# An empty step of a lane moved from behind a tile's second scores to ahead of its first, in a hybrid encoder layer on one Trainium2 core

## The chip, the cores and the metric

The kernel runs on one core of a Trainium2 chip. The core has a matrix engine (TensorE, PE in the profile; its weight loads are PEld), a vector engine (VectorE, DVE), a scalar engine (ScalarE, ACT), a general engine (GpSimd, POOL) and one that issues transfers (SyncE, SP). Each works through its own list of instructions in order and waits at semaphores for the others. The metric is the device time of one execution in microseconds, lower is better; the time before is the median of three runs.

## The reference

One layer of a bidirectional hybrid encoder, for two request groups (1024 and 256 rows, together ten tiles of 128 rows) with shared weights, in float32:

```
hn = rms_norm(x, norm_g);  proj = hn @ w_in
xbc, z_ssd, dt, q, k, v, z_att, mq, z_mem = split(proj)
# 1. state space group: convolution of width 5 over time, silu, two scans (forward and backward)
xbc   = silu(conv5(xbc));  y = scan(xbc, dt) + scan(reversed) + d_skip * xs
o_ssd = rms_norm(y * silu(z_ssd))
# 2. local attention: 8 heads in 2 key groups, |t - s| <= 128, linear distance penalty, a sink logit
s     = (rms_norm(q) . rms_norm(k)) * d**-0.5 - slope * |t - s|
o_att = softmax_with_sink(s) @ v * silu(z_att)
# 3. attention over a memory of 256 rows
o_mem = softmax(rms_norm(mq) . mk) @ mv * silu(z_mem)
out   = x + concat[o_ssd, o_att, o_mem] @ w_out
```

The changed code is part 2.

## The kernel before, in words

**Two kinds of work.** The large projections are split into two reduced-precision halves and run as three matmuls each. They run in blocks (`block_tok`, lines 258 to 260, one matmul 128 x 512; `block_feat`, lines 293 to 295, one matmul 128 x 320). Everything between the projections (local attention `attn`, memory attention, the scans `ssd_up` and `ssd_down`) is written as Python generators that stand in two queues, the lanes: `attn` in lane 0, the scans in lane 1.

**What sets the order.** After each unit of a projection block, `pump` adds the block's rates to what each lane is owed, and for every whole step owed it advances the generator at the lane's head to its next `yield`. A `yield` with nothing ahead of it is an empty step: it lets the projections and the other lane go on. A step's instructions are put into the program behind the last split of a weight tile (`marks`). The order on each engine follows from there by a list scheduler; at run time each engine keeps it. `some_left` puts in the taps of the convolution one at a time in the same way.

**Local attention, `attn(t)`, t = 0 to 9.** Tiles 0 to 3 run beside the `x` blocks (`block_feat`), which also produce the convolution's input; tile 4 beside the second `q` block, 5 to 7 beside further `block_tok` blocks, 8 and 9 later. One call norms its query tile `q`, splits it (`qh`), turns it by four matmuls per half into a PSUM tile `pq` (L671), and ACT copies that out as `qT` (L673); there are two, one for each half of the heads. Then a step issues the load of the gate `z`, and the four head pairs follow:

- `scores(rr)`: two score tiles `psc`, each of two matmuls (L689 and L690); DVE adds the distance penalty and takes the row minimum (L691, `lg` and `nm`); ACT takes the exponential (L695); DVE the reciprocal and the scaling (L697, L698).
- `turn_(rr)`: PE transposes the two scaled tiles into `ppt` (L628), after a small POOL memset that opens them as `lgw` (L635); ACT copies them out as `pT` (L713).
- `values()`: the product with the values.

**Buffers.** `pq`, `psc`, `ppt` and the small tiles of the scans share the PSUM pool `mix` with three buffers. The projections use the pool `acc` with five.

**The convolution's buffers.** For each pair of feature blocks, `ev_conv` opens a buffer `u`: DVE copies the carried columns in (L391) and clears the gaps (L392, L393). Taps run on ACT and DVE (L357, L362), then ACT's L365 and DVE's L368 finish `u`, and SyncE stores it (L372 and L373, to `xbc_d`). The tag of these buffers has two of them, so the next `u` opens over a stored one.

## Time and profile before

| what | value |
|---|---|
| median of 3 runs | 1779.43 us (1779.38 to 1779.74) |
| the profiled execution | 1784.13 us |
| its span | 1782.4 us, 31990 instructions, mean clock of PE 0.999 |
| PE busy | 1766.5 us (99%) |
| DVE busy | 1247.7 us (70%) |
| ACT busy | 919.5 us (52%) |
| POOL busy | 554.6 us (31%) |
| transferred | 301.16 MB, mean 169 GB/s |

The span is the time between the first and last instruction of the profiled execution; its own time includes what lies around the span. The busy time of PE is the sum over its matmuls, and what is missing to the span are its waits. In rows of the timeline the first number is the start in us from the span's start, the second the duration; in brackets stand the idle time of the engine ahead of it and what ended it. In rows of waits the numbers are the total, how often, and the longest, in us.

### The profile page before, as it was taken

How to read it: one execution, taken by the hardware profiler on the slowest of the kernel's cores; microseconds unless marked ns; L12 is line 12 of the kernel's file. 1: busy time of each engine (PE TensorE's matmuls, PEld its weight loads, DVE VectorE, ACT ScalarE, POOL GpSimd, SP SyncE). 2: the span in 40 equal slices, each digit the busy share in tenths (PEclk: the TensorE clock that was granted, in tenths of full speed). 3: DMA queues.
4: the chain of work that ended last, by engine and by line, in shares of the span. 5: the costliest groups of instructions: out<-in, count | busy, mean ns of one | idle time of the engine just before them, and what ended most of it. 6: DMA issues, size and time to landing. Idle time of an engine off the chain costs nothing. (4 is left out here: it accounts for less than half of the span.)

```text
span 1782.4 us, 31990 instructions
## 1 busy us (share of the span) xinstructions
PE 1766.5 (99%) x11046; PEld 1610.4 (90%) x11046; DVE 1247.7 (70%) x2348; ACT 919.5 (52%) x2049; POOL 554.6 (31%) x980
## 2 busy tenths in 40 slices
PE   9999999999999999999999999999999999999999
PEld 7888999999998999999889988887988888899999
DVE  5595788888868878777765675557777654766665
ACT  5554555554434766666455565645447533533333
POOL 0105798999810100001000100011110000058775
PEclk9999999999999999999999999999999999999999
DMA  9553444445446644553545655557777764644442
GB/s 303 189 183 114 146 149 145 144 141 169 123 145 202 191 136 131 150 168 98 182 121 187 181 160 160 165 170 246 220 244 236 247 191 145 220 142 148 148 142 78
DMA packets 208210, 301.16 MB, mean 169 GB/s; under 512 B 19568, under 2 KB 86192, under 8 KB 208048
## 3 DMA queue, kind: packets, MB, share of 16 engines
q1 hardware_dynamic: 207904, 299.06, 54.6%
q8 instruction: 87, 1.43, 0.3%
q14 instruction: 75, 0.61, 0.1%
q10 hardware_dynamic: 144, 0.06, 0.0%
HBM read 236.36 MB, written 62.69 MB: 168 GB/s over the span
## 5 line engine op out<-in xcount | busy, mean ns | idle before, releaser
L207 DVE TENSOR_TENSOR wl<-wraw,wh 128x512 fp32r<-128x512 f32 (+1 forms) x480 | 347.2, 725 | 229.4 <-ACT wh L206 212.5
L206 ACT ACTIVATE wh<-wraw 128x512 fp32r<-128x512 f32 (+1 forms) x480 | 292.1, 613 | 291.8 <-PE acc L260 156.1
L258 PE MATMUL acc<-wh,xH 128*128 128x512 f32 (+1 forms) x1088 | 418.9, 385 | 0.4 <-DVE v_all L337 0.4
L259 PE MATMUL acc<-wl,xH 128*128 128x512 f32 (+1 forms) x1088 | 410.4, 377 | 0.2
L260 PE MATMUL acc<-wh,xL 128*128 128x512 f32 (+1 forms) x1088 | 410.6, 378 | 0.0
L258 PEld LDWEIGHTS acc<-wh,xH 128*128 128x128 f32 x1088 | 204.6, 188 | 37.3 <-issue 2.7
L260 PEld LDWEIGHTS acc<-wh,xL 128*128 128x128 f32 x1088 | 204.8, 188 | 36.7 <-issue 0.2
L259 PEld LDWEIGHTS acc<-wl,xH 128*128 128x128 f32 x1088 | 204.9, 188 | 36.3 <-DVE wl L207 1.5
L293 PE MATMUL acc<-xH,wh 128*128 128x320 f32 x640 | 202.5, 316 | 0.6 <-DVE zs L309 0.6
L206 ACT ACTIVATE sh<-ws 128x384 fp32r<-128x384 f32 x176 | 91.5, 523 | 210.6 <-POOL ws L1256 111.1
L295 PE MATMUL acc<-xH,wl 128*128 128x320 f32 x640 | 199.1, 311 | 0.0
L294 PE MATMUL acc<-xL,wh 128*128 128x320 f32 x640 | 198.1, 310 | 0.0
L207 DVE TENSOR_TENSOR sl<-ws,sh 128x384 fp32r<-128x384 f32 x176 | 124.9, 713 | 97.0 <-ACT sh L206 94.7
L1256 POOL TENSOR_TENSOR ws<-wraw 128x128 f32<-128x128 f32 x176 | 112.8, 641 | 205.9 <-DMA wraw<-in_w_in_pairs_dram 93.7
L293 PEld LDWEIGHTS acc<-xH,wh 128*128 128x128 f32 x640 | 120.2, 188 | 3.6 <-issue 2.4
L1256 POOL TENSOR_TENSOR ws<-wraw,ws 128x128 f32<-128x128 f32 x176 | 117.9, 670 | 13.8
L294 PEld LDWEIGHTS acc<-xL,wh 128*128 128x128 f32 x640 | 120.2, 188 | 1.3 <-issue 1.0
L295 PEld LDWEIGHTS acc<-xH,wl 128*128 128x128 f32 x640 | 120.2, 188 | 0.7 <-issue 0.7
L1256 POOL TENSOR_TENSOR ws<-ws,wraw 128x128 f32<-128x128 f32 x176 | 117.1, 665 | 0.0
L1256 POOL TENSOR_TENSOR wraw<-wraw 128x128 f32<-128x128 f32 x176 | 111.4, 633 | 13.7
L635 POOL MEMSET lgw<- 128x1 f32 x40 | 3.9, 98 | 310.4 <-DVE lg L698 202.4
L362 DVE SCALAR_TENSOR_TENSOR c<-u,vec,c 128x638 f32<-128x638 f32 (+1 forms) x96 | 90.1, 940 | 9.0 <-ACT c L357 8.7
(440 smaller groups left out, 3957.5 us busy)
## 6 DMA issues: line engine op xcount, KB each, us to landing
wraw<-in_w_in_laid_dram SPq DMA_DIRECT2D x176, 256.0 KB, 2.9
wraw<-in_w_in_pairs_dram SPq DMA_DIRECT2D x112, 256.0 KB, 2.7
wraw<-in_w_out_laid_dram SPq DMA_DIRECT2D x64, 256.0 KB, 3.2
wraw<-in_w_out_pairs_dram SPq DMA_DIRECT2D x64, 256.0 KB, 2.7
rf<-ac SPq DMA_DIRECT2D x40, 256.0 KB, 3.9
rb<-ac SPq DMA_DIRECT2D x40, 256.0 KB, 4.9
wraw<-in_w_mem_laid_dram SPq DMA_DIRECT2D x32, 256.0 KB, 4.7
xst<-in_x_sample_dram SPq DMA_DIRECT2D x20, 256.0 KB, 5.0
```

Source lines behind the costliest of these rows:

```text
L206: a = A.activation(h, raw, AF.Copy)
L207: b = V.tensor_sub(l, raw, h.bitcast(F32))
L258: T.matmul(ps[t][:, :n], sh, h[:, :n], start=(k_ == 0), stop=False)
L259: T.matmul(ps[t][:, :n], sh, l[:, :n], start=False, stop=False)
L260: T.matmul(ps[t][:, :n], sl, h[:, :n], start=False, stop=(k_ == KT - 1))
L293: T.matmul(o, sh, cur["H", q][:, m, c], start=(k == 0), stop=False)
L294: T.matmul(o, sh, cur["L", q][:, m, c], start=False, stop=False)
L295: T.matmul(o, sl, cur["H", q][:, m, c], start=False, stop=(k == KT - 1))
L362: V.scalar_tensor_tensor(out=c[0], in0=u[:, k:k + n], scalar=cw[k], in1=c[0], op0=ALU.mult, op1=ALU.add)
L635: G.memset(w.bitcast(F32)[(slice(None),) + tuple(slice(n - 1, n) for n in shape)], 0.0)
L1256: G.tensor_tensor(out=o, in0=x, in1=y, op=op)
```

## The change

In `attn` one `yield` is added ahead of `scores(0)`, and one of the two behind `scores(1)` is taken out. The number of steps of a tile stays the same. Both `scores(0)` and `scores(1)` come one step later against all that is ahead of them, and `turn_(0)` and everything behind it stay where they were.

```
+        yield
         scores(0)
         yield
         scores(1)
-        yield
         yield
         turn_(0)
         yield
```

PE, in query tile 1 beside an `x` block, before: the transposes of the second half (`pq`), the scores of the first head pair (`psc_8400` with the first `qT`, `psc_8404` with the second), and the projection's matmuls between them.

```order
L671 MATMUL pq_8381<-identr_84,qh_8346 128x128 x4
L689 MATMUL psc_8400<-kT_6116,qT_8344 128x384
L690 MATMUL psc_8400<-kL_6117,qT_8344 128x384
L293 MATMUL acc_8196<-xH2_7129,wh_8429 128x320
L294 MATMUL acc_8196<-xL2_7130,wh_8429 128x320
L295 MATMUL acc_8196<-xH2_7129,wl_8430 128x320
L689 MATMUL psc_8404<-kT_6116,qT_8386 128x384
L690 MATMUL psc_8404<-kL_6117,qT_8386 128x384
```

PE in the same place, now: between these transposes and the rows below stand 24 matmuls of the projection. `psc_8443` and `psc_8447` are the scores of the first head pair, `psc_8466` and `psc_8470` those of the second.

```order
L689 MATMUL psc_8443<-kT_6116,qT_8344 128x384
L690 MATMUL psc_8443<-kL_6117,qT_8344 128x384
L689 MATMUL psc_8447<-kT_6116,qT_8386 128x384
L690 MATMUL psc_8447<-kL_6117,qT_8386 128x384
L689 MATMUL psc_8466<-kT_6116,qT_8344 128x384
L690 MATMUL psc_8466<-kL_6117,qT_8344 128x384
L293 MATMUL acc_8196<-xH2_7129,wh_8485 128x320
L689 MATMUL psc_8470<-kT_6116,qT_8386 128x384
L690 MATMUL psc_8470<-kL_6117,qT_8386 128x384
```

The first pair has moved behind the 24 matmuls, which stood between the two pairs before, and the two pairs are now adjacent but for one matmul.

DVE, in the same place, before: the end of a convolution buffer (`u_8189`, L368), the first softmax (`lg_8397`), and the opening of the next buffer (`u_8672`, L391).

```order
L368 SCALAR_TENSOR_TENSOR u_8189<-u_8189,c_8337 128x646
L691 ISA lg_8397,nm_8399<-pdist_6128,psc_8400,nsink_6131 128x384
L691 ISA nm_8399 128x1
L207 TENSOR_TENSOR wl_8558<-wraw_8555,wh_8557 128x512
L691 ISA lg_8397,nm_8399<-pdist_6128,psc_8404,nsink_6131 128x384
L691 ISA nm_8399 128x1
L697 RECIPROCAL den_8408<-den_8408 128x2
L698 TENSOR_SCALAR lg_8397<-lg_8397,den_8408 128x384 x2
L391 COPY u_8672<-carry_96 128x4
```

DVE, now, with the first softmax as `lg_8440` and the second as `lg_8463`:

```order
L368 SCALAR_TENSOR_TENSOR u_8189<-u_8189,c_8337 128x646
L207 TENSOR_TENSOR wl_8558<-wraw_8555,wh_8557 128x512
L391 COPY u_8672<-carry_96 128x4
L392 MEMSET u_8672 128x4
L393 MEMSET u_8672 128x2
L691 ISA lg_8440,nm_8442<-pdist_6128,psc_8443,nsink_6131 128x384
L691 ISA nm_8442 128x1
L207 TENSOR_TENSOR wl_8564<-wraw_8561,wh_8563 128x512
L691 ISA lg_8440,nm_8442<-pdist_6128,psc_8447,nsink_6131 128x384
L691 ISA nm_8442 128x1
L691 ISA lg_8463,nm_8465<-pdist_6128,psc_8466,nsink_6131 128x384
```

The opening of the next buffer stood behind the first softmax and now stands ahead of it; the second softmax's first two operations have come up against the first's.

More of the change, by code (lines that the diff above doesn't have):

```diff
@@ L725, in values @@
             V.tensor_mul(oT, po, z)
+        yield
         scores(0)
@@ L729, in attn @@
         scores(1)
-        yield
         yield
```

## The prediction

> **What bounds the kernel now.** I read the page first: busy times, the slices, the chain that ended last.

> ```profile
> span 1782.4 us, 31990 instructions
> ...
> PE 1766.5 (99%) x11046; PEld 1610.4 (90%) x11046; DVE 1247.7 (70%) x2348; ACT 919.5 (52%) x2049; POOL 554.6 (31%) x980
> ...
> PE   9999999999999999999999999999999999999999
> ...
> PEclk9999999999999999999999999999999999999999
> ...
> PE 26%; DMA 1%; issue 1%; DVE 1%; POOL 0%; ACT 0%; SPq 0%; POOLq 0%; DVEq 0%; ACTq 0%
> ```

> TensorE (PE) is the bound from end to end, at full clock in every slice: 1766.5 of 1782.4 us busy, which leaves 15.9 us. The change adds and removes no instruction, so it can move only those 15.9 us, by mending waits or by making new ones. The second view is therefore the waits of PE alone.

> ```profile
> PE psc L689 <- ACT qT L673: 2.5, 1, 2.5
> PE pst L914 <- ACT fh L928: 1.8, 1, 1.8
> ...
> PE pmt L628 <- DVE mpr L805: 1.5, 1, 1.5
> ...
> PE pd L1094 <- DMA ydT<-yd: 0.7, 1, 0.7
> ...
> PE ppt L628 <- ACT pT L713: 0.3, 1, 0.3
> ...
> PE psc L689 <- DVE xs L909: 0.2, 1, 0.2
> ```

> The operations that the change moves are the score matmuls (`psc`, L689 and L690) and, relative to them, the turns (`ppt`, L628). Their waits sum to 2.5 + 0.2 + 0.3 = 3.0 us, and 2.5 of that is one stall. Nothing else in the list belongs to the moved code, apart from `pd`, whose data come later out of the same lane. So the third view is that stall, on PE, in query tile 1.

> ```profile
> 678.38 0.46 PE L671 MATMUL pq<-identr,qh 128*128 128x128 f32 x4
> 678.67 0.41 PE L689 MATMUL psc<-kT,qT 128*128 128x384 f32 x1
> ...
> 679.10 0.31 PE L293 MATMUL acc<-xH,wh 128*128 128x320 f32 x1
> 679.25 0.31 PE L294 MATMUL acc<-xL,wh 128*128 128x320 f32 x1
> 679.39 0.31 PE L295 MATMUL acc<-xH,wl 128*128 128x320 f32 x1
> 682.16 0.44 PE L689 MATMUL psc<-kT,qT 128*128 128x384 f32 x1 [2.46 <-ACT qT L673]
> 682.44 0.34 PE L690 MATMUL psc<-kL,qT 128*128 128x384 f32 x1
> ```

> The second head's query is transposed into `pq` at 678.38; the score matmul that needs it stands only five instructions later, and PE sits for 2.46 us. The copy of the transpose out of PSUM is late because ScalarE (ACT) is:

> ```profile
> 679.56 0.63 ACT L977 ACTIVATE rb<-rb 128x512 f32<-128x512 f32 x1 [1.57 <-DVE rb L976]
> ...
> 680.38 0.73 ACT L365 ACTIVATE u<-c 128x646 f32<-128x646 f32 x1
> 681.02 0.61 ACT L206 ACTIVATE wh<-wraw 128x512 fp32r<-128x512 f32 x1
> 681.54 0.57 ACT L673 ACTIVATE qT<-pq 128x512 fp32r<-128x512 f32 x1
> ```

> The bias at L977 waited 1.57 us, and `qT` behind it in the queue ends at 681.54 + 0.57 = 682.11.

> **Step 1: the added step ahead of the first scores, tile 1.** In the new order 24 matmuls of the projection stand between `pq` and the first score. A matmul of this block starts 0.147 us after the one before (679.10, 679.25, 679.39), so the first score stands at 678.67 + 24 x 0.147 = 682.20. It uses the first head, ready long before. The second score, which needs the late `qT`, stands 0.35 us on, at 682.55, against 682.11. ACT's order up to `qT` is unchanged, so the 2.46 us go.

> **What is late next.** Both pairs of scores now follow each other directly, and PSUM's pool `mix` has three buffers: the fourth score waits until VectorE (DVE) has read the first (L691). How that runs when DVE is free is shown by tile 4, where the pairs are adjacent already:

> ```profile
> 1022.95 0.34 PE L689 MATMUL psc<-kT,qT 128*128 128x384 f32 x1
> ...
> 1024.24 0.38 PE L689 MATMUL psc<-kT,qT 128*128 128x384 f32 x1
> ```
> ```profile
> 1023.50 0.61 DVE L691 CUSTOM_DVE_ANT_0 lg<-pdist,psc,nsink 128x384 f32<-128x384 bf16 x1 [5.15 <-PE psc L690]
> ```

> The fourth score comes 1.29 us after the first, as DVE ends (1023.50 + 0.61 = 1024.11), with no wait marked. In tile 1 the fourth score is thus due at 682.20 + 1.29 = 683.5. But DVE is not free there. Its rows before:

> ```profile
> 681.14 0.83 DVE L368 SCALAR_TENSOR_TENSOR u<-u,c 128x646 f32<-128x646 f32 x1 [0.91 <-ACT u L365]
> 681.89 0.61 DVE L691 CUSTOM_DVE_ANT_0 lg<-pdist,psc,nsink 128x384 f32<-128x384 bf16 x1
> ...
> 685.29 0.16 DVE L391 COPY u<-carry 128x4 f32<-128x4 f32 x1
> 685.39 0.06 DVE L392 MEMSET u<- 128x4 f32 x1
> ```

> L391 opens a new convolution buffer `u`. It reuses the one that L368 finishes at 681.97, so it must wait until that one's two stores (L372, L373 on SyncE's queue) have landed. Before, it stood behind the first softmax and found them landed, at 685.29 with no wait. After, it stands ahead of the first L691, and everything of the softmax is queued behind it. The stores' rows:

> ```profile
> 682.37 0.42 SPq L373 DMA_DIRECT2D xbc_d<-u  x1
> ```
> ```profile
> L373 SPq DMA_DIRECT2D xbc_d<-u x1: 425/425/425, 682.4 to 682.4; - x1
> ...
> DMA to landing us min/median/max: 2.0/2.0/2.0
> ```

> This store landed 2.0 us after issue, at 684.4. The copy holds DVE for 0.10 us (685.29 to 685.39), L691 takes 0.61, so the first buffer is free at 685.1 and the fourth score waits 685.1 - 683.5 = 1.6 us. That such waits are real shows in tile 0, where the same copy held DVE up:

> ```profile
> 633.80 0.17 DVE L391 COPY u<-carry 128x4 f32<-128x4 f32 x1 [1.34 <-DMA xbc_d<-u]
> ```

> SyncE's order around these stores is the same in both versions, so the issue at 682.37 stands. Term 1: -2.46 + 1.6 = -0.9 us. Its ends: the wait may vanish wholly (-2.5). Or the store takes as long as the longest of its line:

> ```profile
> DMA to landing us min/median/max: 1.9/2.5/4.8
> ```

> At 4.8 us the fourth score waits 2.8 us longer, 4.4 us, and the term is +1.9; at the median of 2.5, 2.1 us, and it is -0.4. I take the value of the very store in the trace.

> [...]

> **Step 2: first scores a step later in the other tiles.** Tile 3 has a small gap of the same kind, and loses it, since there too the new order puts 24 matmuls between the transposes and the first score:

> ```profile
> 777.94 0.31 PE L294 MATMUL acc<-xL,wh 128*128 128x320 f32 x1
> 778.30 0.44 PE L689 MATMUL psc<-kT,qT 128*128 128x384 f32 x1
> ```

> 0.36 us where 0.147 is due: -0.2. Tile 8 has less, and tile 9 some under the two readings of 0.2 and 0.3 in the waits; together I take -0.4 for step 2, between 0 and the 0.2 + 0.2 + 0.3 + 0.2 = 0.9 that all of them would give.

> **Step 3: fourth scores that come early, tiles 0, 2, 3, 8.** Counting the matmuls of the new order at their intervals, the fourth score follows the first after 2.5, 2.4, 1.3 and 1.6 us, where before it was 3.9 to 8.1. Tile 4 shows that 1.3 suffices if DVE is free. If it has just begun a long operation, such as

> ```profile
> 679.34 0.89 DVE L362 SCALAR_TENSOR_TENSOR c<-u,vec,c 128x646 f32<-128x646 f32 x1
> ```

> PE waits up to 0.9. DVE is busy 70% of the span, but tiles 0 and 2 have 1.1 us of room beyond tile 4's 1.29 (2.4 - 1.29) and cover one such operation. So the exposure is tiles 3 and 8 and, for tile 2, a second operation in the queue. Ends 0 and 4 x 0.9 = 3.6; I take +0.4.

> **Step 4: the removed step, scores to turns.** The distance on PE from the first scores to their turn falls from 7.7 to 9.4 us to about 5.0 us in tiles 0, 1, 3, from 9.4 and 14.3 to 6 and 6.6 in tiles 8 and 9; from the second scores to theirs it falls to 5.4, 4.8 and 3.8 in tiles 6, 7, 9. In tile 4 the distance was short already:

> ```profile
> 1027.84 0.22 PE L628 MATMUL ppt<-identr,lgw 128*128 128x128 f32 x1
> ```

> 1027.84 - 1022.95 = 4.89 us with no wait, DVE busy with L207 between. So 4.8 to 5.0 is hidden, barely; 3.8 in tile 9 is for narrower scores. Ends 0 and +0.9 (one L362 in front) at each of these six places, 5.4; I take +0.2, since tile 4 shows nothing lost. In tile 1 the stalled fourth score holds the turn back as well, so the softmax keeps its time.

> **Step 5: what follows in tile 9.** Its outputs leave about half a step later and end in the transfer that PE waited 0.7 us for (`pd`, above). Against the gaps counted in step 2 I set 0, ends -0.7 and +0.7. DMAs of the lanes (the query fetch, `z`, `yd`) keep their order but for neighbours; no term.

> **Sum.** -0.9 - 0.4 + 0.4 + 0.2 = -0.7 us. The profiled execution is the one to which this belongs; its own time was 1784.13 us, 4.7 above the median of the three runs, 1779.43. I take the difference over unchanged: 1779.43 - 0.7 = 1778.7. What a measurement of this kernel can tell from no change is about 0.2%, 3.6 us: below 1775.9 is faster, above 1783.0 slower.

> **Rivals.**
> - **The store lands late.** All as above, but the copy at L391 in tile 1 waits 4.8 us for the stores. +1.9 in term 1 instead of -0.9: 1781.5. For it: the line's own longest landing, and tile 0's wait. Against it: 2.0 in this very place, and the transfers around it stand in the same order. A stall of 4.4 us would be longer than any PE wait of the list, the clock under it is not shown here. [...]
> - **The stall goes for good.** DVE reaches the first L691 ahead of the copy, or the copy finds the buffer free: -2.5 in term 1, and 1779.43 - 2.5 - 0.4 + 0.6 = 1777.1; with every small gap gone too (0.9 of step 2, 0.7 of step 5, nothing for steps 3 and 4), -4.1 and 1775.3, which is measurable. Against it: the new order on DVE has the copy ahead of L691.
> - **Slower: the softmax no longer fits under the matmuls.** One mechanism: DVE, 70% busy, is a long operation late at the turns of step 4. Six places at 0.9 are 5.4, and 1779.43 - 0.9 - 0.4 + 0.4 + 5.4 = 1783.9. It decides from a mean of about 0.8 us a place. For it: 4.8 to 5.0 leaves little; against it, tile 4.

> **How the numbers follow.** My forecast, within a microsecond or so of 1778.7: 0.56. Store late: 0.14, of which 0.01 beyond 0.2%. Stall gone: 0.18, of which 0.09, with the small gaps, beyond 0.2%. Softmax exposed: 0.12, of which 0.09 beyond 0.2%. So faster 0.09, slower 0.10, same 0.81. The range leaves out the measurable gain below 1775.9 and, above, the exposed softmax but for a little: it ends at 1781.9, the late store's 1781.5 with 0.4 over. The likeliest case's own range is 1777.5 to 1779.9.

> **What would show it.** Right: no wait on `qT` in the list of PE; in tile 1 the copy L391 on DVE with a wait of about 1.8 us for `xbc_d<-u`, and a score matmul at L689 with 1 to 2 us; tiles 4 to 7 unchanged; PE idle near 15 us. Wrong: several new waits of `ppt` on DVE or POOL, a larger wait at `pd`, or no wait at L391.

## The result, and the profile after

The changed kernel takes 1777.08 us (median of 22 runs, 1775.87 to 1780.11), against 1779.88 us for the kernel before in the same comparison (22 runs, 1777.06 to 1784.16). The ratio is 0.9982, 95% interval 0.9975 to 0.9989: 3.2 us less, just inside the 0.2% that I took for no change, where the forecast was 0.7 us less. In a second comparison on another occasion the ratio was 0.9977 (0.9968 to 0.9986). One execution of the kernel before, in a later comparison, took 4096 us and is left out of every count below. The gain is clear of the noise and four to five times what I had summed up.

The page of the profile after, and PE's waits:

```profile
span 1776.2 us, 31998 instructions
...
PE 1763.4 (99%) x11046; PEld 1608.4 (91%) x11046; DVE 1245.6 (70%) x2348; ACT 918.9 (52%) x2049; POOL 554.6 (31%) x980
```
```profile
PE pst L914 <- ACT fh L928: 1.6, 1, 1.6
...
PE psc L689 <- DVE nm L691: 1.4, 1, 1.4
PE pmt L628 <- DVE mpr L805: 1.4, 1, 1.4
...
PE pd L1094 <- DVE nm L691: 0.2, 1, 0.2
```

The wait of a score for `qT` (2.5 us) is gone; in its place a score waits 1.4 us for `nm`, the last instruction of L691. The 0.7 us at `pd` have shrunk to 0.2. And PE was busy 3.1 us less (1766.5 before) with the same 11046 matmuls, so some of them took less time. That is not in any list of waits, and the experiments had to find it.

Tile 1 on PE, after:

```profile
680.20 0.34 PE L689 MATMUL psc<-kT,qT 128*128 128x384 f32 x1
...
682.98 0.44 PE L689 MATMUL psc<-kT,qT 128*128 128x384 f32 x1 [1.42 <-DVE nm L691]
```

The store that the copy waits for, after:

```profile
L373 SPq DMA_DIRECT2D xbc_d<-u x1: 423/423/423, 679.9 to 679.9; - x1
...
DMA to landing us min/median/max: 2.2/2.2/2.2
```

Tile 1 on DVE, after:

```profile
678.68 0.83 DVE L368 SCALAR_TENSOR_TENSOR u<-u,c 128x646 f32<-128x646 f32 x1 [0.91 <-ACT u L365]
679.43 0.68 DVE L207 TENSOR_TENSOR wl<-wraw,wh 128x512 fp32r<-128x512 f32 x1
682.17 0.17 DVE L391 COPY u<-carry 128x4 f32<-128x4 f32 x1 [2.06 <-DMA xbc_d<-u]
...
682.30 0.61 DVE L691 CUSTOM_DVE_ANT_0 lg<-pdist,psc,nsink 128x384 f32<-128x384 bf16 x1
```

This is the chain of the prediction, link for link: the store is issued at 679.9 and lands 2.2 us later, DVE stands 2.06 us at the copy until then, the first L691 comes behind it, and the fourth score behind that.

To see where the rest came from I measured stretches of PE's program: the time from the start of one matmul to the start of another at the same two places in the order. Below, in us, by the time of the kernel before; of each kernel there are two profiles (the second ones come from the experiments).

| stretch | before | before, 2nd | after | after, 2nd |
|---|---|---|---|---|
| 628 to 660 (tile 0) | 32.06 | 32.11 | 31.54 | 31.66 |
| 660 to 690 (tile 1) | 30.20 | 31.77 | 29.23 | 29.47 |
| 722 to 760 (tile 2) | 37.94 | 38.09 | 38.15 | 38.17 |
| 760 to 790 (tile 3) | 30.01 | 30.03 | 29.85 | 29.84 |
| 850 to 860 (no local attention) | 9.97 | 10.03 | 8.30 | 8.23 |
| 1000 to 1195 (tiles 4 to 7) | 194.91 | 194.81 | 195.04 | 194.96 |
| 1195 to 1240 (tile 8) | 45.22 | 44.93 | 44.96 | 44.94 |
| 1240 to 1330 (tile 9) | 89.88 | 89.72 | 89.18 | 89.25 |

Most rows repeat within 0.15 us. Two do not fit a story of waits alone: 1.57 us more in tile 1 of the second profile of before, and 1.7 us at 850 to 860, where the change moved nothing.

### The profile page after: what moved, and what is told of

Its sections match the earlier page's. It is cut to its first block, busy times and chain, and to the rows that moved or that the text cites. A ratio compares the mean times of both kernels' runs of the same rounds, so it can differ in the third digit from the quotient of the medians.

```text
span 1776.2 us, 31998 instructions
## 1 busy us (share of the span) xinstructions
PE 1763.4 (99%) x11046; PEld 1608.4 (91%) x11046; DVE 1245.6 (70%) x2348; ACT 918.9 (52%) x2049; POOL 554.6 (31%) x980
## 2 busy tenths in 40 slices
PE   9999999999999999999999999999999999999999
## 5 line engine op out<-in xcount | busy, mean ns | idle before, releaser
L207 DVE TENSOR_TENSOR wl<-wraw,wh 128x512 fp32r<-128x512 f32 (+1 forms) x480 | 346.7, 724 | 227.6 <-ACT wh L206 218.7
L206 ACT ACTIVATE wh<-wraw 128x512 fp32r<-128x512 f32 (+1 forms) x480 | 292.2, 613 | 294.3 <-PE acc L260 155.8
L293 PE MATMUL acc<-xH,wh 128*128 128x320 f32 x640 | 202.8, 317 | 0.0
L206 ACT ACTIVATE sh<-ws 128x384 fp32r<-128x384 f32 x176 | 91.3, 523 | 207.6 <-POOL ws L1256 109.6
L294 PE MATMUL acc<-xL,wh 128*128 128x320 f32 x640 | 198.6, 310 | 0.0
L295 PE MATMUL acc<-xH,wl 128*128 128x320 f32 x640 | 198.4, 310 | 0.0
L207 DVE TENSOR_TENSOR sl<-ws,sh 128x384 fp32r<-128x384 f32 x176 | 124.9, 713 | 98.1 <-ACT sh L206 94.5
L293 PEld LDWEIGHTS acc<-xH,wh 128*128 128x128 f32 x640 | 120.1, 188 | 2.6 <-issue 2.1
L294 PEld LDWEIGHTS acc<-xL,wh 128*128 128x128 f32 x640 | 120.2, 188 | 1.5 <-issue 1.2
L295 PEld LDWEIGHTS acc<-xH,wl 128*128 128x128 f32 x640 | 120.2, 188 | 0.7 <-issue 0.7
L362 DVE SCALAR_TENSOR_TENSOR c<-u,vec,c 128x638 f32<-128x638 f32 (+1 forms) x96 | 90.0, 939 | 9.9 <-ACT c L357 9.5
```

The source lines that it names most:

```text
L206: a = A.activation(h, raw, AF.Copy)
L207: b = V.tensor_sub(l, raw, h.bitcast(F32))
L293: T.matmul(o, sh, cur["H", q][:, m, c], start=(k == 0), stop=False)
L294: T.matmul(o, sh, cur["L", q][:, m, c], start=False, stop=False)
L295: T.matmul(o, sl, cur["H", q][:, m, c], start=False, stop=(k == KT - 1))
L362: V.scalar_tensor_tensor(out=c[0], in0=u[:, k:k + n], scalar=cw[k], in1=c[0], op0=ALU.mult, op1=ALU.add)
```

## The experiments

My theory when they began: PE gains what its waits lose, tile 1 first (2.5 to 1.4 us), and what lies elsewhere is the profiles' own. Rivals: the change works through something else in the lanes, and tile 1 is only its trace; or the fourth score waits for the softmax and not for the copy.

**The kernel before, a second profile** (no edit).

> The kernel before once more, for a second profile. Between the two profiles the span shrank by 6.2 us, of which the stretches beside the local attention account for about 2.3 (tile 0 -0.5, tile 1 -1.1, tile 2 +0.4, tile 3 -0.2, tiles 4 to 7 +0.1, tile 8 -0.3, tile 9 -0.7); the rest lies where no instruction was moved, above all 1.7 at 850 to 860 us and 0.8 at 590 to 600. Theory: that rest is the first profile's own, and goes here too: 850 to 860 takes 8.3 to 8.5 us less the tenth that its wait costs more, 590 to 600 about 9.3, while PE's wait for qT in tile 1 stays at 2.3 to 2.6. Rival: the rest belongs to the change (transfers that fell otherwise), and this run repeats 9.97 and 10.06 us there.

Half right, and the miss was the find. 590 to 600 us took 9.23, as after; that 0.8 was the first profile's own. But 850 to 860 us took 10.03, not 8.3, and the clock rows say why. Columns: stretch, its length, PE's busy time, PE's granted clock, the transfers' share and rate. First before, then after (second profile of before below):

```profile
853.00:856.00 3.00, 1.45 (x11) 0.91 0.61 209
856.00:859.00 3.00, 3.00 (x15) 0.52 0.90 240
859.00:862.00 3.00, 3.00 (x26) 1.00 0.69 204
```
```profile
850.00:853.00 3.00, 1.59 (x13) 1.00 0.59 174
853.00:856.00 3.00, 3.00 (x26) 1.00 0.98 294
856.00:859.00 3.00, 3.00 (x26) 1.00 0.81 217
```

In both the same wait of `pmt` stands there, 1.5 and 1.4 us. Behind it, before ran at half clock (15 matmuls in 3 us instead of 26), and after did not. The second profile of before, by its 10.03 us, did so as well, and had the same behind its wait for `qT`, which is the 1.57 us of the table:

```profile
676.00:679.00 3.00, 1.44 (x11) 1.00 0.73 227
679.00:682.00 3.00, 2.07 (x10) 0.80 0.63 203
682.00:685.00 3.00, 3.00 (x16) 0.63 0.25 84
685.00:688.00 3.00, 3.00 (x22) 1.00 0.05 11
```

Read in stretches of 1 us, such a piece is 3.4 us of half clock: 0.5 in two or three of them and the rest in those beside, 1.7 us of clock lost. So a new theory: a wait of PE costs its length and, by chance, about 1.7 us more for a piece of half clock right behind it. (The wait for `qT` repeated, at 2.5 us.)

**Tile 1 alone, tiles 8 and 9 alone.**

```
         if t == 1:        # the other run: t > 7
             yield
         scores(0)
         yield
         scores(1)
         if not t == 1:    # the other run: not t > 7
             yield
         yield
```

> The change in query tile 1 alone; the other tiles keep the old order. Theory: the 2.5 us wait on qT is replaced by one of about 1.4 us behind the copy at L391, so the stretch of tile 1 is 1.0 to 1.2 us shorter and the time falls by about 1.1 us, a third of the whole change. Rival (tile 1 carries the change): the whole gain of 2 to 4 us is there already, because what follows in the other lanes falls otherwise.

> The change in query tiles 8 and 9 alone. Theory: tile 9's wait at pd for its transfer (0.7 us) goes or shrinks and tile 8 loses 0.2 to 0.3, so 0.7 to 1.1 us less there, and tile 1 keeps its 2.5 us wait on qT. Rival: the wait at pd varies by itself from run to run with the transfer's landing, and the stretches of tiles 8 and 9 are as before within 0.3 us.

Tile 1 alone: 0.9994 (0.9985 to 1.0004), 1.1 us less by the ratio, as the theory said, though the interval also holds no change; it reaches down to 2.7 us less, so the time alone does not rule out that tile 1 carries all. The profile speaks against that: the 2.5 us wait is replaced by 1.7 and the tile 1 stretch is 29.43, but tiles 0 and 9 did not get shorter (32.4 and 89.84). Tiles 8 and 9 alone: 1.0001 (0.9991 to 1.0011), inconclusive as a time. In its profile the wait for `qT` is there (2.1 us) and the stretch of tile 9 is 89.23, that of after (89.18 and 89.25), where the three other profiles with the old tile 9 (before twice, tile 1 alone) have 89.72 to 89.88: about 0.6 us belong to tile 9. Tile 8 shows nothing (45.43 here, 44.94 in tile 1 alone with the old tile 8).

**The buffer's opening on POOL, with the change and without it.** Both kernels, the changed and the one before, got this edit:

```
-            V.tensor_copy(u[:, 0:4], carry[:, fc, :])
-            V.memset(u[:, 388:392], 0.0)
-            V.memset(u[:, 648:650], 0.0)
+            G.tensor_copy(u[:, 0:4], carry[:, fc, :])
+            G.memset(u[:, 388:392], 0.0)
+            G.memset(u[:, 648:650], 0.0)
```

> The changed kernel, with the opening of the convolution buffers (L391 to L393) moved from DVE to POOL. PE's order in tile 1 is the same. Theory (the fourth score waits because DVE stands at the copy): DVE no longer stands there, the 1.4 us wait of the score matmul goes to under 0.3, and the time falls by another 1.0 to 1.4 us against the changed kernel, 3.5 to 5 against before. Rival (the fourth score waits for the softmax's own length): the wait stays at 1 us or more. A second rival: POOL now stands at the copy, and the memsets that open lgw behind it hold the turns up; then waits of ppt of 0.5 us and more appear and take the gain back.

> The kernel before, with the opening of the convolution buffers (L391 to L393) on POOL, as in the fourth run of the first batch, which took 4.3 us off with the change. Theory: in the old order nothing of PE stands behind that copy, so the wait for qT in tile 1 stays at about 2.5 us, and the time is within 1 us of before. Rival: the copy on POOL brings its gain whatever the order, by freeing DVE elsewhere, and the time falls by 1.0 to 2.0 us here too.

With the change: 0.9975 (0.9965 to 0.9985) of before, 4.4 us less. The wait at the fourth score is not in the list any more, tile 1's stretch is 27.67 us, 1.6 to 1.8 less than after. In time that step is not shown apart: the interval also holds the changed kernel's 0.9977 and 0.9982. DVE is free when the first score comes, and it is POOL that stands at the copy:

```profile
679.66 0.83 DVE L368 SCALAR_TENSOR_TENSOR u<-u,c 128x646 f32<-128x646 f32 x1 [0.92 <-ACT u L365]
680.47 0.69 DVE L207 TENSOR_TENSOR wl<-wraw,wh 128x512 fp32r<-128x512 f32 x1
682.08 0.61 DVE L691 CUSTOM_DVE_ANT_0 lg<-pdist,psc,nsink 128x384 f32<-128x384 bf16 x1 [0.91 <-PE psc L690]
```
```profile
682.90 0.45 POOL L391 COPY u<-carry 128x4 f32<-128x4 f32 x1 [4.84 <-DMA xbc_d<-u]
```

DVE now waits for the score (0.91 us) and not the score for DVE. No wait of `ppt` came in its place, so the second rival fell too. Without the change: 0.9991 (0.9981 to 1.0001), the wait for `qT` there at 2.0 us. The copy's place matters little in the old order, as expected, with one exception: tile 0's stretch fell to 31.60, the value of after (31.54, 31.66). In the old order DVE stands at such a copy in tile 0 and everything behind it comes late, down to a score of the third pair:

```profile
641.41 0.39 PE L689 MATMUL psc<-kT,qT 128*128 128x256 f32 x1 [0.17 <-DVE xs L909]
```

In the run with tiles 8 and 9 alone, whose tile 0 is also the old one, the copy waited longer, 2.53 us instead of 1.34, and the score 1.05 instead of 0.17:

```profile
633.66 0.17 DVE L391 COPY u<-carry 128x4 f32<-128x4 f32 x1 [2.53 <-DMA xbc_d<-u]
```
```profile
641.26 0.38 PE L689 MATMUL psc<-kT,qT 128*128 128x256 f32 x1 [1.05 <-DVE xs L912]
```

After, DVE does a tap of L362 ahead of the copy, waits 0.41 us there, and no score waits:

```profile
631.29 0.17 DVE L391 COPY u<-carry 128x4 f32<-128x4 f32 x1 [0.41 <-DMA xbc_d<-u]
```

So the change makes PE wait for this copy in tile 1 and takes a wait for the same one away in tile 0.

**PE kept busy in the wait.** The kernel before, with ten matmuls without use in the place of the 2.5 us wait:

```
                 st = qT[kv][:, rr * P:(rr + 1) * P]
+                [T.matmul(ps, identr, kT[:, 0, :512], start=True, stop=True)
+                 for _ in range(10 if (t, rr, kv) == (1, 0, 1) else 0)]
```

> The kernel before, with ten matmuls of 128 x 512 without use ahead of the second score of tile 1, in the place where PE waits 2.5 us for qT. Their 2.3 us fit into the wait, so the work behind it comes no later and no earlier; only PE is busy instead of idle. Theory (a long wait of PE costs its length and, by chance, a stretch of half clock of 3.4 us that costs 1.7 us more, as one of three profiles with the old tile 1 shows right behind this wait, at 680 to 684 us): no half clock at 680 to 690 us, fewer runs with a mean clock under 1.000 than the 16 of 28 of the kernel before, and a time 0.5 to 1.0 us less, though the wait is the same. Rival: half clock comes from elsewhere (the load, the other waits), and the share of runs with it and the time are as before, or 0.1 to 0.3 above for matmuls that run over.

0.9993 (0.9984 to 1.0002), medians 1779.17 and 1781.12. The ten matmuls took 2.49 us and PE then still waited 0.88 us for `qT`. They did not fit wholly: three matmuls of the projection moved behind the second score, and the stretch of tile 1 is about 0.8 us longer than in the first profile of before. So nothing came earlier, and the work behind came later. What changed is the clock. The profile shows it full behind the wait,

```profile
676.00:679.00 3.00, 3.00 (x18) 1.00 0.48 176
679.00:682.00 3.00, 2.12 (x14) 1.00 0.73 253
682.00:685.00 3.00, 3.00 (x21) 1.00 0.32 87
```

which alone says little, since two of the four profiles with the unfilled wait (the first of before, and tiles 8 and 9 alone) have no half clock there either. The runs say more: 2 of 11 had a mean clock under 1.000, against 24 of 33 of the kernel before beside it. Among runs at a mean clock of 1.000 the two kernels are equal, medians 1778.91 (9 runs) and 1779.01 (9 runs). By the time alone the interval still just holds no change; the counts and the equal medians at full clock are what speaks for the theory, and its rival (the same share of runs) fell.

**Each half of the change.** Only the added step (`yield` ahead of the first scores, both behind the second kept), and only the removed one:

```
+        yield                 # only in the first
         scores(0)
         yield
         scores(1)
         yield
-        yield                 # only in the second
         turn_(0)
```

> The first half of the change alone: a step ahead of the first scores, and both steps behind the second scores kept, so that a tile takes one step more. Theory: PE's wait for qT in tile 1 goes as in the changed kernel, and the two pairs of scores stay apart, 24 matmuls between them, so that no wait of a score for a buffer takes its place: the stretch of tile 1 is 2 us shorter or more, if the later tiles (ten steps more in the lane in all) cost nothing. Price of that unknown; time 1774 to 1778 if they cost nothing. Rival: the gain comes from the removed step (the tile's end no later), and without it the lane runs late, the flush ahead of the second group's keys has more to do, and the time is 1780 or more.

> The second half of the change alone: one step behind the second scores less, nothing ahead of the first. Theory: qT is as late as before where the first scores stand right behind its transposes, so the wait of about 2.5 us in tile 1 stays or moves to another tile, and the time is within 1 us of before, or up to 2 above it where turns come too early. Rival: the removed step brings the gain (everything behind a tile's scores comes earlier), and the time is 1776 to 1778 with the wait still there.

The added step alone has the whole gain in time: 0.9981 (0.9972 to 0.9990). From 600 to 850 us PE has no wait in the list at all, and at `pmt` 0.2 instead of 1.4. It loses some of it again at 1200 to 1330 us, where the lane comes ten steps late; rows of that stretch:

```profile
PE pd L1095 <- DMA ydT<-yd: 1.4, 1, 1.4
PE psc L689 <- ACT qT L673: 1.3, 1, 1.3
PE ppt L628 <- DVE lg L698: 0.7, 1, 0.7
```

The removed step alone is 1.0007 (0.9998 to 1.0016): no gain. Its waits show what a tile with too little room does; `qT` is nearly gone (0.3), since scores and transposes fell otherwise, and what PE waits for are the buffers and, at `pd`, a transfer:

```profile
PE psc L689 <- DVE nm L691: 2.1, 2, 1.7
PE pd L1093 <- DMA ydT<-yd: 1.8, 1, 1.8
PE psc L689 <- DVE xs L908: 1.6, 1, 1.6
...
PE ppt L628 <- DVE nm L691: 0.9, 1, 0.9
```

I had expected the `qT` wait to stay; it did not, and the rival (a gain from the removed step) fell as well. Among runs at a mean clock of 1.000 it is even 2.3 us slower than before (medians 1781.27, 6 runs, and 1779.01). From this and the waits of the added step alone I take it that removing the step serves the late tiles, by keeping them from coming later.

**Both kept where there is room.** The step ahead in all tiles, the second step behind kept in tiles 0 to 3, or 0 to 7:

```
+        yield
         scores(0)
         yield
         scores(1)
-        yield
+        if t < 4:             # the other run: t < 8
+            yield
         yield
```

> A step ahead of the first scores in every tile as in the changed kernel, but the second step behind the second scores is kept in tiles 0 to 3 and goes out only in tiles 4 to 9. Theory: the first half of the change alone had no wait of PE from 600 to 1200 us above 0.2 (no qT, no fourth score, and 0.2 instead of 1.4 at pmt), and lost it again in tiles 8 and 9 (3.6 us of waits at pd, qT, ppt) where the lane was late; so this one has no wait above 0.3 in tiles 0 to 3 and at pmt, at most 0.7 in all in tiles 8 and 9, and takes 1.5 to 3 us less than the changed kernel, with fewer half clocks. Rival: the four steps more are enough to make tiles 8 and 9 late, the waits there stay at 2 us or more, and the time is that of the changed kernel within 1 us.

> The same with the second step kept in tiles 0 to 7 and out in tiles 8 and 9. Theory: waits up to 1200 us as in the run before; in tiles 8 and 9 the lane is eight steps late instead of four, so the waits there lie between that run's and the 3.6 us of ten steps. Rival: only the order inside tiles 8 and 9 counts, not how late they are; then this run and the one before have the same waits there and the same time within 0.5 us.

> The changed kernel once more, for a second profile and its time on the same chip as the two others. Theory: PE's wait for the first L691 in tile 1 repeats at 1.3 to 2.3 us, as the store behind the copy lands 1.9 to 2.8 us after its issue; the stretch of tile 0 repeats at 31.5 us and that of tiles 8 and 9's end at 89.2; under a third of the runs have a mean clock below 1.000; the time is 2.5 to 3.5 us under before. Rival: these stretches scatter as much between two profiles of the same kernel as between the kernels, by 0.5 us and more.

Kept in tiles 0 to 3: 0.9966 (0.9954 to 0.9979), 6.1 us less than before and the lowest ratio of all, from five runs (median 1775.94, lowest 1773.12). Against the changed kernel beside it (0.9977) that is 2.0 us less, within the 1.5 to 3 expected, but the two intervals overlap. Its waits:

```profile
PE acc L1290 <- ACT qs L326: 1.7, 2, 0.9
PE warm L1566 <- DVE zero L1564: 1.3, 1, 1.3
PE psc L689 <- ACT pT L713: 0.5, 1, 0.5
PE pd L1096 <- DMA ydT<-yd: 0.4, 1, 0.4
```

Neither tile 1 nor `pmt` waits, as the theory said; the waits from 1200 to 1330 us sum to 0.9 us (the last two rows) where it allowed 0.7. The fewer half clocks that I expected did not come: four of its five runs had a mean clock under 1.000; in the profile the piece stands at 153 to 157 us, behind the first row. Kept to tile 7: 0.9987 (0.9977 to 0.9996), with 2.3 us at `pd` and 1.1 at `qT`: by these waits lateness counts, not only the order inside a tile. Nine of its 11 runs had a mean clock under 1.000, which its time includes. The changed kernel again: 0.9977, its wait 1.7 us in tile 1 (the copy waited 2.64), stretches as in the table, 2 of 11 runs under a mean clock of 1.000 against 14 of 21 of before. At a mean clock of 1.000 the medians are 1776.80 (9 runs) and 1779.06 (7 runs).

## Why the prediction was right or wrong

**The bound and the main step were right.** PE ends everything, and only its waits (and, as it turned out, its clock) could move. Step 1 said that the wait for `qT` goes and that the fourth score then waits 1.6 us, behind L691, behind the copy at L391, behind a store that lands 2.0 us after its issue: measured 1.4 and 1.7 in two profiles, with the copy waiting 2.06 and 2.64. Term 1 was -0.9; the stretch gave -0.97 and -0.73. The store landed 2.2 us after its issue, where I took the 2.0 of the profile before; for the second profile 2.8 is an estimate, from the copy's start at 682.34 and an issue 1.2 us behind the start of L368 (678.26), as in the first.

**Steps 2 to 4 were small, as said.** Tile 3 gave -0.17 (I had -0.2). Tile 2 is 0.15 longer, with no wait in the list, and no early fourth score waits in tile 3 or 8; that is less than the 0.4 I took. The turns (`ppt`) are not in PE's list of waits after; tiles 4 to 7 are 0.14 longer in all. The slower rival (the softmax exposed) was wrong for this kernel, though its waits are real: the removed step alone has them.

**Two terms were mis-sized.** Step 5, what follows in tile 9, was set to 0, and the stretch of tile 9 measured -0.6. The wait at `pd` explains most of that in the first pair of profiles (0.7 to 0.2 us) but only 0.1 in the second (0.3 to 0.2); where the rest lies was not found. And step 2 had no term for tile 0, while the stretch gave -0.5. It counted the wait of 0.2 us for `xs` to tile 9, but that is the score at 641.41 in tile 0; the 0.3 us at `ppt` is at 1237.0, in tile 8. I had read the copy's wait in tile 0 (1.34 us) as evidence that such waits exist, and not followed it to what stood behind it on DVE, though the same copy carried the argument in tile 1. The stretches that changed sum to -0.5 - 0.85 + 0.15 - 0.17 + 0.14 - 0.6 = -1.8 us, and the runs at full clock differ by 2.3.

**One cost was missing.** The prediction said that the change can move only the 15.9 us in which PE is idle, and it took a wait's price to be its length. But PE's busy time fell too, by 3.1 us. The page of the profile shows PEclk at 9 in all 40 slices, which I quoted as full clock in every slice: a piece of 3 us at half clock is invisible in a slice of 45 us. Where the clock of each run was recorded, 54 of 82 runs of the kernel before (16 of 28, 24 of 33, 14 of 21) had a mean clock under 1.000; after, 7 of 33. By the clock's thousandths, before lost 0.9 pieces a run where the changed kernel beside it lost 0.18; 0.7 pieces of 1.7 us are 1.2 us. With the 2.3 us at full clock that gives 3.5, where the two ratios say 3.2 and 4.1.

This split is inferred from the counts. That a busy PE in the place of the wait makes half clock rarer is shown, by the counts of that run (2 of 11 against 24 of 33). That the wait for `qT` is the only source is not: with it at 2.0 us and more, 70 of 105 runs were under 1.000 (before, the copy on POOL without the change, tiles 8 and 9 alone); with it gone or shorter, 27 of 90; yet in the two kernels that keep both steps in some tiles 13 of 16 were, though no wait of theirs stands in tile 1.

**Luck in the total.** The sum was -0.7 us and the measurement -3.2. The time lies in the range given, 1775.9 to 1781.9, because the range is wide against the sum; the likeliest case's own range, 1777.5 to 1779.9, missed it by 0.4, and the second comparison's 0.23% is beyond the 0.2% that I took for no change. So the mechanism of step 1 was right, and that the rest summed to no more than this was luck.

**The rivals.** The store never landed as late as 4.8 us in this place, and the stall did not go for good; where it does (the copy on POOL) the price I gave, 1.6 us, is about what came off tile 1 (1.6 and 1.8). My 0.01 for a late store beyond 0.2% needs more than its 1781.5 us; no run shows that: the longest single wait of PE in the thirteen profiles is 2.5 us, and the half clock behind such a wait cost about 1.7 us where it came.

## What to carry to other kernels

Price a stall of the bounding matrix engine at more than its length (here about 1.7 us more behind six of the 29 single waits of 1.2 us and over, `warm` left out): look at the granted clock in windows of 1 to 3 us behind each wait, not in the page's slices. When two groups of work are moved against each other, follow every in-order queue through the place, and ask of each small instruction that waits for a transfer (here a copy of four columns that stood 2.06 us) what stands behind it; moving it to an engine with room took 1.6 us off this tile on top of the reordering. Where a step of slack is taken out, look for the tiles that have room for both: by the waits in the profiles, taking it out was of use in the late tiles and a cost in the early ones.

## What the runs showed of the hardware

A wait of PE brought half clock in some profiles and not in others, and not by its length alone. Of the single waits of 2.0 us and more in the thirteen profiles, three of six had half clock right behind (`qT` in two of four, `pst` at 2.4 in one, `pd` at 2.3 not); of those from 1.2 to 1.9 us, the one at the start (`warm`) left out, three of 23, all at `pmt`. In two profiles (the copy on POOL, the step kept in tiles 0 to 3) a piece stood at 152 to 157 us behind two waits that follow each other closely (0.56 and 0.82 us, 0.90 and 0.81). Each piece cost about 1.7 us.
